# One core, three blocks of tokens: a group of gates moved to the start of the middle block, z's product and the stores of x tied to products

## Chip, cores and metric

The kernel runs on one core of one Trainium2 chip. The metric is the device time of one execution in microseconds; smaller is better. Five engines work side by side, each through its own instructions in order: TensorE (PE, with its weight loads PEld), VectorE (DVE), ScalarE (ACT), GpSimd (POOL) and SyncE (SP). Here SP only issues DMA transfers; POOL issues DMA transfers as well and computes a little.

## What is computed

One encoder layer runs over 2048 tokens of a prompt and 64 tokens of a second sequence that brings its own state. Cut to its core:

```python
h = rms_norm(x, g_pre)
vA, bA, cA, zA, q, f, iv, zB, gA, gB = split_cols(h @ w_in)       # ten times 1024 columns
yA = (silu(zA) * bA * causal_conv3(cA * vA)) @ w_a_out
fg = lb + (1 - lb) * sigmoid(f)                                   # 8 heads of 128
S, o = hgrn2_scan(S0, silu(q) * QK_SCALE, 1 - fg, iv, log(fg))    # chunks of 64 tokens
o = o * rsqrt(mean(o * o) + EPS) * g_onorm
yB = (o * silu(zB)) @ w_b_out
x = x + rms_norm((sigmoid(gA) * yA + sigmoid(gB) * yB) @ w_o, g_post)
x = x + (p @ w_ple_proj) * sigmoid(rms_norm(x, g_ple) @ w_ple_gate)
```

All data are fp32. The outputs are x for both sequences, the last two columns of the convolution's input, and the scan's final states.

## The kernel before

**Blocks.** The 2112 tokens are cut into three blocks of 768, 704 and 640 tokens, held with features on partitions. Every block goes through the same stages: the gates (columns gA and gB), `path_b` (eight heads with the scan), `path_a`, the merge, `out`, then the norms and the final gate. The stages of two blocks interlock: while TensorE works on the first seven groups of gates of the next block (`LEAD = 7`), the norms of the block just finished (`final_norm`, L1405) run on the other engines. Then come the finished block's final gate (`final_gate`, L1458) and after it the next block's `path_b` (L1213).

**Products.** An fp32 matrix is split into a high part `hi` (cast on ACT) and a rest `lo` (DVE, L226), and each matrix product is made of three fp32r matmuls (L442 to L444: hi by hi, hi by lo, lo by hi). `sgroup` (L427) works two 128-column blocks of weights against the halves of the token block in seven products instead of eight, with sums S1 to S4 of weight tiles as operands. A product is 12 matmuls, a group 84.

**Weights and their sums.** `combined` (L341) provides the operands. The first time that a pair of weight blocks is used, four raw tiles are loaded (L236), four sums are made on DVE (L352), split, and stored together with their `lo` parts, for later blocks (L331 for S, L280 for `low`). Later uses load sums and `lo` parts again (L236 and L274). Pools: 5 buffers for raw tiles, 4 for `hi`, 4 for `lo`, 3 for sums `s`. All loads, and these stores too, go through SP's queue, except that `stores[0]` is set to POOL's queue when block 1 begins (L1641). The last group of gates (gB, column blocks 6 and 7) has no sums after block 0, where it runs through another routine; block 1 is the first to make them.

**Gates.** `gates` (L868) is a generator of eight groups; each group writes two gate tiles, which POOL stores (L866). Seven groups are drawn before the final gate of the block before. In blocks 1 and 2 the eighth is drawn in `path_b`, after the preparation of head 5 (`hd == KH + 1`, L1223 to L1226), with SP as the queue of its stores for that moment.

**Hooks.** After every product, `hook` (L313) runs one entry of a list: a step of the attention, of a norm, or nothing. In `path_b` of blocks 1 and 2 a head is given 14 entries, one for each product of the next head's preparation, and 21 where the group of gates stands between. Steps of a head's attention sit at entries 2 to 10; at 11 the normalized output `o` goes out through the buffer `to` (L1055), at 14 it is read back in another order (L1060), and at 21 `scale_o` (L1209) multiplies it into z (L1211) and POOL stores z (L1218, kind `o`).

**Order on an engine.** The source gives dependencies and a rough order. A scheduler in the framework decides where an instruction stands in its engine's queue. `paced` (L300) adds a dependency on `last[0]`, the last matmul emitted so far, to an instruction.

**Norms.** `final_norm` loads x (L1418), adds the normalized `out` (L1436, L1437), takes the second mean square (L733, `rms` L715), and then, in eight steps `j` that stand two products apart, stores x of column block `j` for the final gate (L1447), multiplies by g_ple (L1454) and splits into `h2` (L226). `final_gate` reloads x and p (L1319), merges (L1463, L1464) and stores y (L1465). The large tiles come from one ring of 48 buffers (`rt`, L154).

Of the kernel before, what the change touches and what calls it, by code (L numbers as in the profile page):

```python
# [14 lines left out]
ALU = mybir.AluOpType  # L15
# [5 lines left out]
KB = D // P  # L21
KH = KB // 2
NH = 8
# [70 lines left out]
def hybrid_step(  # L94
# [17 lines left out]
    V, A, G, T, SP = nc.vector, nc.scalar, nc.gpsimd, nc.tensor, nc.sync  # L112
# [13 lines left out]
    def nm(s):  # L126
        uid[0] += 1
        return f"{s}_{uid[0]}"
# [12 lines left out]
    def sized(bl, steps):  # L141

        while True:
            with sized_to(bl):
                try:
                    made = next(steps)
                except StopIteration:
                    return
            yield made

    def hn():
        return width[0] // 2

    def rt(n=0, dt=F32):  # L154
        t = ring.tile([P, BN + 2], dt, tag="r", name=nm("r"))
        return t if n is None else t[:, : n or width[0]]
# [10 lines left out]
    def spill(kind, j):  # L167
        return dram.tile([P, BN], F32, tag=f"{kind}{j}", name=nm(kind), bufs=2)[:, : width[0]]
# [56 lines left out]
    def split(src, hi, lo):  # L225
        return A.copy(hi, src).ins, V.tensor_tensor(lo, src, hi.bitcast(F32), ALU.subtract).ins  # L226
# [12 lines left out]
    lows, turn, stores = {}, [0], [SP]  # L239
# [54 lines left out]
    last, hooks, copies, adds, ahead, evicted, freed, powers, means = [None], [], [None], [None], [], [], [], [], []  # L294
# [5 lines left out]
    def paced(dma):  # L300

        tc.add_manual_dep(
            dma.ins, last[0].name, mybir.DependencyInfo(mybir.DependencyClass.Sync, mybir.DependencyReason.DATA), reason="paced"
        )
# [410 lines left out]
    def rms(acc, out, segs, hasten=False):  # L715


        cols = [col_rstd(acc[:, cols_of(sg)], sg["n"]) for sg in segs]
        yield
        for sg, col in zip(segs, cols):  # L720
            if hasten:
                ahead[:] = [V.tensor_copy(out[:, cols_of(sg)], spread(col, sg["n"])).ins]
            else:
                A.copy(out[:, cols_of(sg)], spread(col, sg["n"]))
        yield

    def sum_squares(j, src, acc, n):
        if j == 0:
            A.activation(acc, src, AF.Square)
        else:  # L730
            sq = rt(n)
            A.activation(sq, src, AF.Square)
            V.tensor_tensor(acc, acc, sq, ALU.add)  # L733
# [134 lines left out]
    def gates(bl, hc, kept, first):  # L868


        groups = [(kind, j) for kind in (GA, GB) for j in range(0, KB, 2)]
        for kind, j in groups[: -1 if first else None]:
            outs = [rt(), rt()]
            n = groups.index((kind, j))
            sgroup(kind * 8 + j, kind * 8 + j + 1, hc, gate_sink(outs), first, by_k=n == 0 and not first, anew=n < LEAD)
            keep_gates(kept, kind, j, outs)
            yield
# [330 lines left out]

    def scale_o(d, hd):  # L1209
        z = d["z"][:, : d["npair"] * P].rearrange("q (g i a) -> q g i a", i=4, a=32)  # L1210
        V.tensor_tensor(z, d["ot"], z, ALU.mult)  # L1211

    def path_b(bl, hc, first, kept, fills, hs, lead_sums=None):  # L1213


        def keep_z(hd, z):
            kept["o", hd] = spill("o", hd)
            G.dma_start(kept["o", hd], z)  # L1218

        slots, base, d = {}, 0, None  # L1220
        for hd in range(NH):
            d = head_prep(bl, hc, hd, first, hs, d)
            if hd > 0 if first else hd == KH + 1:  # L1223
                queue, stores[0] = stores[0], SP
                next(fills, None)
                stores[0] = queue  # L1226
            assert not hooks
            attn = [head_attn(i, gs, d, hd) for i, gs in enumerate(bl["parts"])]
            keep = partial(keep_z, hd, d["z"])
            piece = lead_sums and partial(next, lead_sums, None)  # L1230

            def at(slot, *steps):
                slots.setdefault(base + slot, []).extend(s if callable(s) else partial(next, s) for s in steps if s is not None)

            if first:
                late = int(hd == 0)
                for g in attn:
                    for slot in (1 + late, 4, 7, 10, 13):
                        at(slot + late + (g is attn[1]), g)
                at(15 + late, keep)  # L1240
                for slot in (15, 17, 19) if hd else (17,):
                    at(slot, piece)
                if hd == NH - 1:
                    for slot in range(22, 70, 4):
                        at(slot, piece)
            else:
                pairs, one = attn[:2], attn[2:]
                for slot, steps in enumerate((pairs[:1], pairs[1:], one, one, pairs, one, pairs, (), one)):
                    at(slot + 2, *steps)
                at(11, partial(turn_o, d))  # L1250
                at(14, partial(read_o, d))
                at(14 + 7, partial(scale_o, d, hd), keep)
            count = 14 + 7 * (first or hd + 1 == KH + 1) if hd + 1 < NH else 1 + max(slots) - base
            for slot in range(base, base + count):
                steps = slots.pop(slot, None)
                hooks.append(partial(each, steps) if steps else None)
            base += count
# [147 lines left out]
    def final_norm(bl, segs, xo, acc, h2, kept, ask_ahead=False):  # L1405

        c = slice(segs[0]["off"], segs[-1]["off"] + hn())
        n = len(segs) * hn()  # L1410
        acc2, rs, rs2 = rt(), rt(), rt()
        xks = []

        def fetch():
            j = len(xks)
            if j < KB:
                xks.append(rt())
                G.dma_start(xks[j][:, c], x_fm[j * P : (j + 1) * P, segs[0]["t0"] : segs[0]["t0"] + n])  # L1418

        for _ in range(2 if bl["last"] else 4):  # L1420
            fetch()
        if kept is not None:
            for j in range(KB):
                sum_squares(j, xo[j], acc, width[0])
                if j % 2:
                    yield
        yield from rms(acc, rs, segs, bl["last"])
        if ask_ahead:
            for _ in range(3):
                fetch()  # L1430
                fetch()
                yield
        for j in range(KB):
            fetch()
            xj = xo[j][:, c]
            V.scalar_tensor_tensor(xj, xj, g_post[:, j : j + 1], rs[:, c], ALU.mult, ALU.mult)  # L1436
            V.tensor_tensor(xj, xj, xks[j][:, c], ALU.add)  # L1437

            for i in (j,) if not bl["last"] else (j - 1,) if 0 < j < KB - 1 else (j - 1, j) if j else ():
                sum_squares(i, xo[i][:, c], acc2[:, c], n)  # L1440
            yield
        yield from rms(acc2, rs2, segs, bl["last"])
        ts = []
        for j in range(KB):
            if kept is not None:
                kept["x", j] = spill("x", j)
                G.dma_start(kept["x", j], xo[j])  # L1447
            if len(h2) <= j:
                h2.append((rt(dt=F32R), rt(dt=F32R)))

            for i in (j, j + 1) if j == 0 else (j + 1,):
                if i < KB:
                    ts.append(rt())
                    V.scalar_tensor_tensor(ts[i][:, c], xo[i][:, c], g_ple[:, i : i + 1], rs2[:, c], ALU.mult, ALU.mult)  # L1454
            split(ts[j][:, c], h2[j][0][:, c], h2[j][1][:, c])
            yield
# [178 lines left out]
    fills = sized(blocks[0], gates(blocks[0], hc, kepts[0], True))  # L1635
    for bi, bl in enumerate(blocks):
        first, kept = bi == 0, kepts[bi]
        width[0] = bl["n"]
        segs = bl["segs"]
        if bi == 1:  # L1640
            stores[0] = G  # L1641
        ahead_of = (*range(W_A, W_A + KH), W_O, W_O + 1) if first else None
        path_b(bl, hc, first, kept, fills, hs if first else None, ahead_of and prepare_sums(ahead_of, pieces=True))
        run(fills)
        a = []
# [18 lines left out]
        mg, xo, h2, acc = [], [], [], rt()  # L1664
# [49 lines left out]
        if nxt:  # L1714
            xo.extend(stages[-1]["mid"])
            fills = sized(nxt, gates(nxt, hc, kepts[bi + 1], False))
# [65 lines left out]
```

## Time and profile before

| what | value |
|---|---|
| time, median of 3 runs | 2559.4 us (2559.28 to 2559.43) |
| the profiled execution's own time | 2566.42 us |
| its span, first to last instruction | 2564.2 us |
| TensorE busy | 2533.4 us (99%) |
| VectorE, ScalarE, GpSimd busy | 70%, 58%, 17% |
| DMA moved | 774.70 MB, mean 302 GB/s |
| block 1: first seven groups of gates; final gate of block 0 | about 894 to 988 us; about 988 to 1054 us |
| block 1: heads; the group of gates after head 5's preparation | about 1054 to 1368 us; about 1250 to 1270 us |
| block 2: first seven groups of gates | about 1737 to 1823 us |

Matmuls overlap in the pipeline, so that a matmul of 0.33 us may follow the one before by half of that. What counts for TensorE is the idle time ahead of a matmul, the number of matmuls in a stretch of time, and the clock that it was granted.

### The profile page before, as it was taken

To read this page: it belongs to the slowest core of one execution; us is meant where nothing else is said; L and a number is where in the kernel's file an instruction comes from. 1 tells how busy PE (TensorE), PEld (TensorE's weight loads), DVE (VectorE), ACT (ScalarE), POOL (GpSimd) and SP (SyncE) were. 2 spreads that over 40 slices of the span, in tenths; PEclk is the share of its full clock that TensorE was granted. 3 is DMA by queue.
4 is the path that set the end of the run, shared out by engine and by line. 5 is a ranking of instruction groups with operands and counts; after the bars stand their busy time and mean duration, and the time that the engine had idled before them with its cause. 6 is when DMAs were issued, how large, how long until landed. Compare 5 with 4: busy or idle time off the path is not lost. (4 is left out here: it accounts for less than half of the span.)

```text
span 2564.2 us, 47005 instructions
## 1 busy us (share of the span) xinstructions
PE 2533.4 (99%) x16070; PEld 2516.8 (98%) x16070; DVE 1795.1 (70%) x3549; ACT 1481.9 (58%) x2876; POOL 448.1 (17%) x793
## 2 busy tenths in 40 slices
PE   9999999999999999999999999999999999999999
PEld 9999999999999999999899999999999999999998
DVE  7888888898868775577574556887437766336967
ACT  6666666554453664466464555666446665446675
POOL 2011121230022021122122221102112221001011
PEclk9999999999999999999999999999999999999999
DMA  8789888998797888888888998998889999989986
GB/s 329 245 283 318 276 291 289 323 367 302 255 342 252 269 306 270 302 275 293 283 276 308 338 389 311 337 303 315 306 302 319 326 328 321 302 300 324 336 273 202
DMA packets 370399, 774.70 MB, mean 302 GB/s; under 512 B 45734, under 2 KB 50528, under 8 KB 370160
## 3 DMA queue, kind: packets, MB, share of 16 engines
q1 hardware_dynamic: 321840, 582.95, 66.8%
q0 software_dynamic: 48320, 188.75, 20.6%
q8 instruction: 126, 2.06, 0.3%
q14 instruction: 113, 0.93, 0.1%
HBM read 559.43 MB, written 212.10 MB: 301 GB/s over the span
## 5 line engine op out<-in xcount | busy, mean ns | idle before, releaser
L442 PE MATMUL pg<-r,hi 128*128 128x320 f32 (+2 forms) x3304 | 1082.3, 328 | 1.7 <-ACT hf L456 1.4
L443 PE MATMUL pg<-r,hi 128*128 128x320 f32 (+2 forms) x3304 | 1067.7, 323 | 0.0
L444 PE MATMUL pg<-r,lo 128*128 128x384 f32 (+2 forms) x2368 | 773.3, 327 | 10.6 <-DMA lo<-low 9.7
L273 ACT CAST hi<-raw 128x512 fp32r<-128x512 f32 x726 | 447.1, 619 | 498.4 <-PE pg L443 172.4
L442 PEld LDWEIGHTS pg<-r,hi 128*128 128x128 f32 x3304 | 623.4, 189 | 2.9 <-ACT hf L456 2.2
L443 PEld LDWEIGHTS pg<-r,hi 128*128 128x128 f32 x3304 | 623.1, 189 | 0.0
L444 PEld LDWEIGHTS pg<-r,lo 128*128 128x128 f32 x2368 | 445.6, 188 | 12.8 <-DMA lo<-low 11.5
L444 PE MATMUL pg<-r,s 128*128 128x320 f32 (+1 forms) x936 | 296.6, 317 | 3.0 <-DMA s<-low 3.0
L594 PE MATMUL pg<-r,hi 128*128 128x320 f32 (+2 forms) x864 | 277.2, 322 | 0.5 <-DVE r L226 0.4
L593 PE MATMUL pg<-r,hi 128*128 128x320 f32 (+2 forms) x864 | 274.9, 322 | 0.0
L226 ACT CAST hi<-raw 128x512 fp32r<-128x512 f32 x252 | 155.3, 620 | 157.8 <-PE pg L443 42.7
L226 DVE TENSOR_TENSOR r<-r,r 128x320 fp32r<-128x320 f32 (+7 forms) x350 | 206.3, 609 | 45.7 <-ACT r L226 44.2
L226 DVE TENSOR_TENSOR lo<-raw,hi 128x512 fp32r<-128x512 f32 x231 | 158.1, 687 | 80.5 <-ACT hi L226 76.3
L226 ACT CAST r<-r 128x320 fp32r<-128x320 f32 (+7 forms) x350 | 183.1, 556 | 43.8 <-DVE r L1333 8.4
L595 PE MATMUL pg<-r,lo 128*128 128x352 f32 (+2 forms) x564 | 181.0, 321 | 1.3 <-DMA lo<-low 1.2
L444 PEld LDWEIGHTS pg<-r,s 128*128 128x128 f32 x936 | 176.3, 188 | 4.0 <-DMA s<-low 3.9
L226 ACT CAST hi<-s 128x512 fp32r<-128x512 f32 x160 | 98.8, 618 | 137.6 <-PE pg L443 109.8
L632 PE MATMUL pg<-r,hi 128*128 128x384 f32 (+2 forms) x512 | 167.0, 327 | 0.2 <-DVE r L226 0.2
L631 PE MATMUL pg<-r,hi 128*128 128x384 f32 (+2 forms) x512 | 165.6, 327 | 0.2 <-ACT hi L273 0.2
L594 PEld LDWEIGHTS pg<-r,hi 128*128 128x128 f32 x864 | 162.2, 188 | 2.1 <-DVE r L226 1.6
L593 PEld LDWEIGHTS pg<-r,hi 128*128 128x128 f32 x864 | 161.2, 188 | 1.3 <-ACT r L226 0.8
L456 ACT COPY hf<-pg 128x352 f32<-128x352 f32 (+2 forms) x354 | 157.4, 446 | 2.6 <-PE pg L444 2.1
(394 smaller groups left out, 4109.6 us busy)
## 6 DMA issues: line engine op xcount, KB each, us to landing
raw<-w_blk SPq DMA_DIRECT2D x578, 256.0 KB, 4.4
raw<-S SPq DMA_DIRECT2D x440, 256.0 KB, 4.7
lo<-low SPq DMA_DIRECT2D x421, 256.0 KB, 4.4
s<-low SPq DMA_DIRECT2D x305, 256.0 KB, 4.6
low<-lo SPq DMA_DIRECT2D x275, 256.0 KB, 4.1
S<-s SPq DMA_DIRECT2D x156, 256.0 KB, 3.9
low<-r POOLq DMA_DIRECT2D x50, 256.0 KB, 5.2
r<-w_blk POOLq DMA_DIRECT2D x48, 256.0 KB, 7.1
```

What stands on the lines that cost most here:

```text
L226: return A.copy(hi, src).ins, V.tensor_tensor(lo, src, hi.bitcast(F32), ALU.subtract).ins
L273: A.copy(hi, raw)
L442: add(hi[:, k, :], xhi, start=start and k == 0, stop=False)
L443: add(hi[:, k, :], xlo, start=False, stop=False)
L444: last[0] = add(lo[:, k, :], xhi, start=False, stop=k == KH - 1).ins
L456: copied = A.copy(got[n], ps[bank])
L593: add(hi[:, k, :], xhi, start=start and k == 0, stop=False)
L594: add(hi[:, k, :], xlo, start=False, stop=False)
L595: last[0] = add(lo[:, k, :], xhi, start=False, stop=k == KH - 1).ins
L631: T.matmul(ps, hi[:, k % 4, :], xhi[:, c], start=k == ks[0], stop=False)
L632: T.matmul(ps, hi[:, k % 4, :], xlo[:, c], start=False, stop=False)
```

## The change

Three edits:

1. **Gates.** In block 1 the eighth group of gates is drawn ahead of head 0's preparation, right behind the final gate of block 0, again with SP as the queue of its stores. No head of block 1 has 21 entries any more. Block 2 keeps its group after head 5's preparation; its stores of sums do not exist, so the switch of queues there is dropped. Block 0 is unchanged.
2. **z.** The product of z and `o` in `scale_o` gets a dependency on the last matmul emitted before it (blocks 1 and 2).
3. **Stores of x.** In `final_norm` of blocks 0 and 1 each store gets such a dependency. At step 0 column blocks 0 and 1 are stored, at step `j` block `j + 1`; the steps stand two products apart.

```diff
     def scale_o(d, hd):
         z = d["z"][:, : d["npair"] * P].rearrange("q (g i a) -> q g i a", i=4, a=32)
-        V.tensor_tensor(z, d["ot"], z, ALU.mult)
+        paced(V.tensor_tensor(z, d["ot"], z, ALU.mult))
...
         slots, base, d = {}, 0, None
+        late_gates = KH + 1 if bl["last"] else None
+        if not first and not bl["last"]:
+            queue, stores[0] = stores[0], SP
+            next(fills)
+            stores[0] = queue
         for hd in range(NH):
             d = head_prep(bl, hc, hd, first, hs, d)
-            if hd > 0 if first else hd == KH + 1:
-                queue, stores[0] = stores[0], SP
+            if hd > 0 if first else hd == late_gates:
                 next(fills, None)
-                stores[0] = queue
...
-            count = 14 + 7 * (first or hd + 1 == KH + 1) if hd + 1 < NH else 1 + max(slots) - base
+            count = 14 + 7 * (first or hd + 1 == late_gates) if hd + 1 < NH else 1 + max(slots) - base
...
         for j in range(KB):
-            if kept is not None:
-                kept["x", j] = spill("x", j)
-                G.dma_start(kept["x", j], xo[j])
+            for i in () if kept is None else (0, 1) if j == 0 else (j + 1,):
+                if i < KB:
+                    kept["x", i] = spill("x", i)
+                    paced(G.dma_start(kept["x", i], xo[i]))
```

## Prediction

> **What bounds the kernel.** First the page's table of engines: busy time, share of the span, instructions.
>
> ```profile
> PE 2533.4 (99%) x16070; PEld 2516.8 (98%) x16070; DVE 1795.1 (70%) x3549; ACT 1481.9 (58%) x2876; POOL 448.1 (17%) x793
> ```
>
> TensorE is busy for all but 30.8 us of the 2564.2 us span, and the change adds and removes no matmul. So it can only win, or lose, idle time of TensorE and time at a lowered clock. Second, the view of waits for PE alone, columns "us in total, times, longest":
>
> ```profile
> PE pg L444 <- DMA lo<-low: 9.7, 4, 6.0
> PE pg L444 <- DMA s<-low: 3.0, 3, 1.3
> PE pg L442 <- ACT hf L456: 1.4, 1, 1.4
> PE pa L1097 <- DVE att L1119: 0.3, 1, 0.3
> PE pa L1111 <- DVE att L1119: 0.2, 1, 0.2
> ```
>
> One wait of 6.0 us stands out; most others are near 1 us. Third, the busy time by stretches of 10 us, first the old place of the moved group (columns: from:to, length, then busy us and instructions of PE, PEld, DVE, ACT, POOL, then PE's granted clock, DMA share, GB/s):
>
> ```profile
> 940.00:950.00 10.00, 10.00 (x64) 10.00 (x63) 6.03 (x10) 6.08 (x11) 1.62 (x3) 1.00 0.94 298
> ...
> 1250.00:1260.00 10.00, 7.03 (x41) 6.21 (x39) 8.85 (x16) 4.92 (x10) 2.92 (x5) 0.96 0.89 291
> 1260.00:1270.00 10.00, 6.62 (x24) 6.63 (x25) 1.70 (x5) 1.11 (x3) 0.71 (x1) 0.52 0.92 322
> ```
>
> The first row is the undisturbed rate in block 1: 64 matmuls in 10 us, 0.156 us each, so a product of 12 takes 1.87 us. In 1250 to 1270 us TensorE idles 2.97 + 3.38 = 6.35 us, and in the second stretch the clock is 0.52: its 24 matmuls fill 6.62 us where 24 x 0.156 = 3.75 would do. The stall costs 6.35 + 2.87 = **9.2 us**, not 6.0.
>
> **The gates' group.** Fourth, the timeline and SP's own waits at that place say why:
>
> ```profile
> 1254.68 0.72 SPq L274 DMA_DIRECT2D lo<-low  x1
> ...
> 1263.38 0.66 PE L444 MATMUL pg<-r,lo 128*128 128x352 f32 x1 [6.03 <-DMA lo<-low]
> ```
>
> ```profile
> SPq L236 <- DVE hf L994: 4.9, 1, 4.9
> SPq L280 <- DVE lo L226: 3.0, 2, 2.7
> ```
>
> TensorE waits from 1257.35 us for the `lo` part of the fifth product's weights. The load left SP at 1254.68 and landed at the end of the wait, 8.7 us later. Four products of 1.87 us before 1257.35 lies the group's start, 1249.9, so the buffer that the load reuses was free at 1251.7: the load left 3.0 us late. Ahead of it in SP's queue stood a load held 4.9 us by DVE's attention work (L994), and stores of `lo` parts held 3.0 us until DVE had made them (L226).
>
> The move takes all that the group issues to about 1054 us: 84 matmuls; seven loads (four raw tiles, three `lo` parts) and eight stores of 256 KB on SP; two stores of 352 KB on POOL; on DVE four sums and four splits. It removes nothing, so the matmuls cost the same. What counts is whether the load waits again. Before, head 0's first group stood there, also one that makes sums (two groups of DVE: busy us, mean ns, idle before; then DVE, SP and PE from the timeline; then the stretch):
>
> ```profile
> L352 DVE TENSOR_TENSOR s<-raw,raw 128x512 f32<-128x512 f32 x80 | 54.8, 686 | 9.5 <-DMA raw<-w_blk 6.6 <-DMA S<-s 2.7
> L226 DVE TENSOR_TENSOR lo<-s,hi 128x512 fp32r<-128x512 f32 x160 | 110.1, 688 | 52.1 <-ACT hi L226 44.5 <-DMA low<-lo 7.4
> ...
> 1053.96 0.69 DVE L226 TENSOR_TENSOR lo<-s,hi 128x512 fp32r<-128x512 f32 x1 [1.40 <-ACT hi L226]
> ...
> 1055.35 0.32 SPq L274 DMA_DIRECT2D lo<-low  x1
> ...
> 1061.56 0.43 PE L444 MATMUL pg<-r,lo 128*128 128x352 f32 x1
> ...
> 1060.00:1070.00 10.00, 9.87 (x61) 9.58 (x61) 4.36 (x9) 4.96 (x9) 1.08 (x2) 1.00 0.99 348
> ```
>
> There the same load left at 1055.35, landed in time but for 0.13 us (10.00 - 9.87), and the clock stayed at 1.00. Its stores went through POOL. In the built program of the changed kernel they stand on SP ahead of this load; the last of them needs the split that DVE ended at 1053.96 + 0.69 = 1054.65, before the load's buffer comes free. DVE is light there: 8 x 0.69 = 5.5 us of the group's work beside the merges. So the stores should not hold SP. Behind it comes head 0's own group with sums, now among gate stores. Bounds for the new place: 0.1 us (this row) and 9.2 us (the stall again). I take **1.0**, near the first: three `lo` loads in each of two groups, each about 6 us under way against 5.6 us of three products, a few tenths late at worst. Heads 5 to 7 lose the seven entries of pause; heads 1 to 4 go without them already. Gain: 9.2 - 1.0 = **8.2 us**.
>
> The clock, weighed: the Trainium skill, "TensorE: Matmul & The Clock Gate", Part 1, says that the clock falls to half after an idle window of about 3.4 us and returns after about as long busy. The row at 1260 agrees (0.52 after 6.03 us); the row at 930 in the next fence (0.83, longest wait 2.5 us) does not fit it. By the page the x stores below would win 3.6 us in block 0 where the rows give 5.3, and the sum would be 2550.1 us.
>
> **The stores of x.** The same view where they stand now, and where they go:
>
> ```profile
> 920.00:930.00 10.00, 8.95 (x57) 8.67 (x56) 7.62 (x12) 3.30 (x6) 1.08 (x2) 1.00 1.03 408
> 930.00:940.00 10.00, 7.50 (x37) 7.21 (x36) 5.86 (x9) 5.97 (x11) 1.63 (x3) 0.83 0.90 326
> ...
> 960.00:970.00 10.00, 10.00 (x64) 10.00 (x63) 7.73 (x11) 6.85 (x13) 0.54 (x1) 1.00 0.81 270
> 970.00:980.00 10.00, 10.00 (x65) 10.00 (x64) 7.88 (x12) 7.11 (x13) 1.08 (x2) 1.00 0.76 250
> ...
> 1770.00:1780.00 10.00, 9.29 (x62) 8.74 (x61) 5.92 (x10) 5.47 (x12) 2.06 (x4) 1.00 0.96 354
> ...
> 1800.00:1810.00 10.00, 10.00 (x70) 10.00 (x69) 7.81 (x13) 7.03 (x14) 0.00 (x0) 1.00 0.89 302
> 1810.00:1820.00 10.00, 10.00 (x71) 10.00 (x70) 7.44 (x11) 7.22 (x15) 1.08 (x2) 1.00 0.94 312
> ```
>
> ```profile
> x<-r POOLq DMA_DIRECT2D x8, 384.0 KB, 6.3
> ...
> POOL x L1447 <- DVE r L1437: 32.4, 13, 5.5
> ...
> 910.80 0.54 POOL L1447 DMA_DIRECT2D x<-r  x1 [3.14 <-DVE r L1437]
> ...
> 942.72 0.54 POOL L1447 DMA_DIRECT2D x<-r  x1 [5.51 <-DVE r L1437]
> ...
> 954.73 0.82 PE L700 MATMUL pa<-ident,cols 128*128 128x128 f32 x6
> 986.86 0.79 ACT L859 ACTIVATE r<-r 128x704 f32<-128x704 f32 x1
> ...
> 1793.68 0.54 PE L700 MATMUL pa<-ident,cols 128*128 128x128 f32 x3 [0.29 <-POOL cols L689]
> 1822.44 0.74 ACT L859 ACTIVATE r<-r 128x640 f32<-128x640 f32 x1 [0.61 <-DVE r L490]
> ```
>
> First row: eight stores, size, median us to landing. The row of waits says that POOL issues a store as soon as DVE has made the block (L1437), long before the steps in which the source puts it: the scheduler had moved them up. Eight of 384 KB, 3.1 MB, fall between 910 and 943 us, beside loads of x; there (920 row) the DMAs are full (408 GB/s, share 1.03) and TensorE waits 1.05 + 2.50 us for weights and runs 37 matmuls in 7.50 us (37 x 0.156 = 5.8): 3.55 + 1.7 = 5.3 us. Block 1 loses 0.7 (1770 row). With the tie the stores stand between the second norm's transposes (L700) and the seventh group's last sigmoid (L859): about 957 to 985 and 1797 to 1823 us. 3.1 MB in 28 us adds 110 GB/s: 270 + 110 = 380 in block 0; 2.9 MB in 26 us make 312 + 110 = 420 in block 1, as full as the 408 row. Price there: from 0 to 5.3 us a block; I take 1.0 in block 0 and 1.5 in block 1, near the 1770 row, which bore eight stores at 0.7. Net 6.0 - 2.5 = **3.5 us**.
>
> The new wait on POOL holds the gates' stores behind it (L866) and at the end the first reload of x (L1319), for which the merge on DVE waits; a store's product is done when its turn comes, so nothing for it. But in the built program the buffers of x blocks 4 and 5 are used again by `h2` (ACT) and that of block 6 by a gate tile (DVE): a store must land within about 4 products, 7.5 us; 6.3 fits.
>
> **z.** The last chain that reaches TensorE, in order of time:
>
> ```profile
> L1211 DVE TENSOR_TENSOR r<-r,r 128x640 f32<-128x640 f32 x16 | 13.2, 826 | 44.7 <-DMA r<-to 44.7
> ...
> 1157.23 0.83 DVE L1211 TENSOR_TENSOR r<-r,r 128x640 f32<-128x640 f32 x1 [3.28 <-DMA r<-to]
> ...
> 1378.37 0.83 DVE L1211 TENSOR_TENSOR r<-r,r 128x640 f32<-128x640 f32 x1 [6.81 <-DMA r<-to]
> ...
> 1379.66 0.50 ACT L923 ACTIVATE r<-hf 128x352 f32<-128x352 f32 x1 [7.11 <-DVE hf L483]
> ...
> 1381.06 0.43 PE L442 MATMUL pg<-r,hi 128*128 128x352 f32 x1 [1.35 <-ACT hf L456]
> ```
>
> Sixteen products of z stand too early on DVE and block it 44.7 us in total; twice that reaches TensorE: after 1378 through L483, ACT and PSUM (1.35 us), after 1157 through the mask copies L1119 (0.26 + 0.23, shown as 0.3 and 0.2). In the built program the tied products stand some 15 instructions later, among the next head's states, when the transfer has landed. Behind them wait those states and mask copies, and on POOL the store of z stands ahead of a reciprocal root of the attention (L689); a late product of TensorE would hold these, but TensorE is the engine that never waits long. Bounds: 1.8 gained; up to 1.4 lost, the dearest such row. I take **1.5**.
>
> **Sum.** 8.2 + 3.5 + 1.5 = 13.2 us. Every reordering shifts the DMA queues, and waits of about 1 us (s<-low: three in 3.0) come up at new places: 2.2 us given back. Forecast -11.0 us. Against the profiled execution that is 2566.4 - 11.0 = 2555.4; its own time stands 7.0 us above the median, so I put the difference on the median: 2559.4 - 11.0 = **2548.4 us**.
>
> **Rivals.**
> 1. *The stall goes along with the group* (the move doesn't do what it is placed for): SP's stores hold the `lo` load once at the new place. For it: the load has no slack there (0.13 us late already). Against it: DVE's splits ended before the load left. 8.2 falls away: -5.0 + 2.2 = -2.8, 2556.6 us.
> 2. *Two stalls instead of one* (slower): two groups with sums follow each other, and the stores of the first hold SP for the loads of both. It decides where the `lo` loads leave SP 3 us or more after the buffer is free, as at 1254.68. Price 2 x 9.2 - 9.2 = +9.2, with x and z -5.0 and +2.2 given back: +6.4, 2565.8 us. For it: both use SP and the same four `lo` buffers. Against it: head 0's stores go through POOL.
> 3. *The peak of x only moves*: the 420 GB/s in block 1 and 380 in block 0 cost what the old places did: 3.5 falls away, -7.5, 2551.9 us.
> 4. *Nothing comes back*: all three gains in full, 9.2 + 6.0 + 1.8 = 17.0: 2542.4 us.
>
> **Chances.** Forecast 0.55, rival 1 0.16, rival 2 0.12, rival 3 0.09, rival 4 0.08. A measurement of this kernel tells about 0.2% (5.1 us) from no change. Faster by more: 0.52 + 0.08 + 0.08 = 0.68; within: 0.03 + 0.16 + 0.01 = 0.20; slower 0.12. The range leaves out rival 2 and half of rival 4: 2542 to 2562 us.
>
> **What would show it.** Right: no wait of 6 us and no clock of 0.52 near 1260; at 1054 to 1082 us waits of under 1 us in all; 920 to 940 us at 64 matmuls a stretch; L1211 hardly waiting for `r<-to`; DMA rows near 1800 to 1820 above 400 GB/s. Wrong: a clock under 0.9 between 1054 and 1085 or 957 and 990 us, or ACT waiting for `x<-r`.

## The result, and the profile after

The changed kernel takes 2544.8 us (2541.6 to 2548.5); the kernel before, beside it on the same chip, takes 2559.3 us (2558.0 to 2560.3). The ratio is 0.9946 [0.9934, 0.9959], and 0.0054 x 2559.3 = **13.8 us less** (10.5 to 16.9). The forecast was 11.0 us less, 2548.4 us. The profiled execution of after took 2544.6 us, with a span of 2542.7 us. Against the span of before that is 21.5 us less, half as much again as the medians give, because the profiled execution of before stood 7.0 us above its median.

The page's table of engines of after, in the columns known from before:

```profile
PE 2527.4 (99%) x16070; PEld 2514.8 (99%) x16070; DVE 1794.5 (71%) x3549; ACT 1482.2 (58%) x2876; POOL 446.7 (18%) x793
```

The number of instructions is the same on every engine. TensorE is busy for 6.0 us less; 2.9 and 1.7 of these are the time at a lowered clock that the prediction read in the rows of 1260 and 930 us, and the rest is not followed. It idles for 2542.7 - 2527.4 = 15.3 us where 30.8 stood. The waits of PE alone (us in total, times, longest):

```profile
PE pa L700 <- POOL cols L689: 2.9, 5, 0.8
PE pg L444 <- DMA lo<-low: 2.0, 3, 1.0
...
PE pg L444 <- DMA s<-low: 0.7, 1, 0.7
```

The loads of `lo` cost 2.0 us instead of 9.7, those of `s` 0.7 instead of 3.0, and the wait for L456 is gone. The busy time by stretches of 10 us, first at the old place of the x stores and at their new one, then at the new and at the old place of the moved group:

```profile
920.00:930.00 10.00, 10.00 (x64) 10.00 (x63) 9.11 (x13) 7.36 (x13) 1.08 (x2) 1.00 0.85 275
930.00:940.00 10.00, 10.00 (x65) 10.00 (x64) 6.84 (x11) 5.95 (x11) 1.07 (x2) 1.00 0.82 275
970.00:980.00 10.00, 10.00 (x63) 10.00 (x62) 9.14 (x15) 7.09 (x12) 1.62 (x3) 1.00 0.98 342
1050.00:1060.00 10.00, 9.63 (x60) 9.34 (x59) 5.86 (x11) 4.66 (x9) 2.62 (x5) 1.00 0.90 328
...
1250.00:1260.00 10.00, 10.00 (x68) 10.00 (x67) 8.54 (x24) 6.90 (x13) 3.16 (x5) 1.00 0.91 308
1260.00:1270.00 10.00, 10.00 (x71) 9.98 (x70) 4.36 (x13) 3.57 (x8) 1.31 (x2) 1.00 1.01 351
...
1800.00:1810.00 10.00, 10.00 (x64) 10.00 (x63) 1.56 (x3) 2.34 (x5) 2.13 (x4) 1.00 1.01 393
```

Where the 920 and 930 rows of before had 57 and 37 matmuls, there are 64 and 65, and the clock is 1.00. The stretch from 1250 to 1270 us has no idle time. The moved group idles for 0.37 us in all, and 393 GB/s in block 1's new place of x cost nothing. On POOL, the stores now wait for products:

```profile
POOL x L1451 <- PE pg L444: 28.6, 10, 3.3
```

(L1451 is L1447 of before; the edits add three or four lines.) These agree with what the prediction said would show it right, and no wait of L1211 for `r<-to` is listed any more. One sign did not come: the DMA rows at 1800 to 1820 us, named as above 400 GB/s, are 393 and 299, and the peak of 403 stands ten us earlier.

### The profile page after: what moved, and what is told of

Read it like the earlier page. It is cut to its first block, busy times and chain, and to the rows that moved or that the text cites. A ratio compares the mean times of both kernels' runs of the same rounds, so it can differ in the third digit from the quotient of the medians.

```text
span 2542.7 us, 47020 instructions
## 1 busy us (share of the span) xinstructions
PE 2527.4 (99%) x16070; PEld 2514.8 (99%) x16070; DVE 1794.5 (71%) x3549; ACT 1482.2 (58%) x2876; POOL 446.7 (18%) x793
## 3 DMA queue, kind: packets, MB, share of 16 engines
q8 instruction: 126, 2.06, 0.3%
## 4 chain that ended last, share of the span: by engine, by line
PE 91%; issue 3%; DVE 3%; DMA 2%; ACT 0%; POOL 0%; SPq 0%; DVEq 0%; ACTq 0%; POOLq 0%
PE pg L442 20%; PE pg L444 20%; PE pg L443 20%; PE pg L594 4%; PE pg L593 4%; PE pg L595 4%; PE pg L633 3%; PE pg L632 3%; PE pg L631 3%; PE pa L1125 1%; PE pa L1165 1%; DMA lo<-low 1%; PE pa L1167 1%; PE pa L1111 1%; PE pa L1110 1%
## 5 line engine op out<-in xcount | busy, mean ns | idle before, releaser
L226 ACT CAST hi<-raw 128x512 fp32r<-128x512 f32 x252 | 155.3, 620 | 159.3 <-PE pg L443 41.9
L226 DVE TENSOR_TENSOR r<-r,r 128x320 fp32r<-128x320 f32 (+7 forms) x350 | 205.9, 607 | 45.4 <-ACT r L226 44.4
L226 DVE TENSOR_TENSOR lo<-raw,hi 128x512 fp32r<-128x512 f32 x231 | 157.8, 686 | 73.4 <-ACT hi L226 69.9
L226 ACT CAST r<-r 128x320 fp32r<-128x320 f32 (+7 forms) x350 | 182.8, 556 | 42.6 <-DVE r L1336 8.3
L226 ACT CAST hi<-s 128x512 fp32r<-128x512 f32 x160 | 98.9, 618 | 144.6 <-PE pg L443 116.9
L456 ACT COPY hf<-pg 128x352 f32<-128x352 f32 (+2 forms) x354 | 157.2, 446 | 2.1 <-PE pg L444 1.7
```

Of the source, the lines that this page charges most:

```text
L456: copied = A.copy(got[n], ps[bank])
```

## Experiments

**Theory.** Each of the three terms acts at its own place, so that single edits give their own part and the parts add up: gates about 8 us, x 3.5, z 1.5. **Rivals:** the parts don't add up, since a stall that goes uncovers the next; the gates' stall is made by their own stores in SP's queue, so that another queue would do as well as another place; the x stores gain by being spread or tied, not by their place, or they pay at the new place for what they save; z is hidden. Three groups of four kernels each ran with the kernel before beside them (medians of before 2559.92, 2560.72 and 2558.94 us). A difference in us is that of the ratio, with its 95% interval; the ratio is close to that of the means, and the difference of two medians can be up to 1.6 us off it.

### The parts one by one

**Gates alone** (the first edit on the kernel before):

```diff
+        late_gates = KH + 1 if bl["last"] else None
+        if not first and not bl["last"]:
+            queue, stores[0] = stores[0], SP
+            next(fills)
+            stores[0] = queue
...
```

> Only the group of gates of the middle block is moved; z and the stores of x as before. Theory A (three separate stalls, each removed by its own edit, sizes as in the sum): -8 us against the kernel before, no wait of 6 us at 1250 to 1270 us, no clock of 0.52 there, under 1 us of wait at the new place. Theory B (the gain is one thing, the move, and the ties bring nothing): -13 to -15 us here. Theory C (the stall comes and goes between executions, so the profile oversized it): -3 to -5 us.

2552.34 us, ratio 0.9967 [0.9954, 0.998]: **-8.4 us** (-11.8 to -5.1). The stretches of its trace at the x stores' old place and at the group's old place:

```profile
920.00:930.00 10.00, 7.94 (x50) 7.65 (x49) 7.99 (x11) 5.58 (x10) 2.16 (x4) 1.00 1.03 407
930.00:940.00 10.00, 10.00 (x53) 10.00 (x54) 6.28 (x9) 5.03 (x9) 1.08 (x2) 0.83 1.01 379
1250.00:1260.00 10.00, 10.00 (x65) 9.98 (x64) 8.48 (x28) 8.23 (x13) 3.91 (x6) 1.00 0.72 243
```

The gates' stall is gone and that of x stays as it was. At the new place 0.57 us are waited. The term of the sum was 8.2.

**Stores of x alone** (the third edit on the kernel before):

```diff
-            if kept is not None:
-                kept["x", j] = spill("x", j)
-                G.dma_start(kept["x", j], xo[j])
+            for i in () if kept is None else (0, 1) if j == 0 else (j + 1,):
+                if i < KB:
+                    kept["x", i] = spill("x", i)
+                    paced(G.dma_start(kept["x", i], xo[i]))
```

> Only the stores of x are tied and stand one step earlier in the source. Theory A: -3.5 us (2 to 5.5), 920 to 940 us back at 64 matmuls in 10 us, the 6 us wait at 1263 us still there. Theory B: within 1 us of the kernel before. Theory C (the full DMAs only move to 1790 to 1820 us): waits for s<-low or lo<-low of 2 us or more there, time within 1.5 us of before.

2552.87 us, ratio 0.9975 [0.9966, 0.9985]: **-6.4 us** (-8.7 to -3.8). Its stretches at the old place, at the new one, and at the gates:

```profile
920.00:930.00 10.00, 10.00 (x64) 10.00 (x63) 9.11 (x13) 7.34 (x13) 1.08 (x2) 1.00 0.83 282
...
960.00:970.00 10.00, 10.00 (x64) 10.00 (x64) 8.21 (x13) 6.82 (x13) 2.16 (x4) 1.00 1.04 395
...
1250.00:1260.00 10.00, 6.62 (x32) 6.62 (x33) 4.07 (x7) 2.40 (x4) 0.79 (x1) 0.83 0.99 358
...
1800.00:1810.00 10.00, 10.00 (x68) 10.00 (x67) 6.32 (x10) 6.67 (x12) 1.08 (x2) 1.00 1.04 406
```

The gates' stall stays. At the new places the DMAs are as full as at the old one (395 and 406 GB/s, shares of 1.04), and TensorE waits for nothing. Counting matmuls from the start of the trace, this profile gains 5.6 us on before between the 5200th and the 5600th matmul (block 0's stores) and 2.6 us between the 10400th and the 11200th (block 1's); 2.7 us of its lead stand ahead of any edit and differ from run to run.

**z alone** (the second edit on the kernel before), and **all but z** (the changed kernel without this edit):

```diff
-        V.tensor_tensor(z, d["ot"], z, ALU.mult)
+        paced(V.tensor_tensor(z, d["ot"], z, ALU.mult))
```

> Only z's product is tied. Theory A: -1.5 us (0.5 to 2); L1211 waits for r<-to under 5 us in total instead of 44.7; no wait of 1.35 us for ACT hf L456; the 6 us wait at 1263 us still there. Theory B: within 0.5 us of before, L1211's waits gone all the same.

> The changed kernel without the tie of z. If the tie of z is worth nothing measurable (as it was alone), the time is that of the changed kernel, -13 to -15 us against the kernel before. If it is worth the 1.5 us of the sum once the other stalls are gone, -12 to -13 us, with TensorE waiting 1 to 1.5 us for ACT hf L456 near the end of the middle block's heads.

z alone takes 2559.90 us, ratio 0.9999 [0.9991, 1.0008]: -0.3 us (-2.3 to +2.0). In the waits of DVE the row of L1211, 44.7 us in before, is gone, and PE's wait for L456 too. What PE still waits for with z alone:

```profile
PE pg L444 <- DMA lo<-low: 8.3, 5, 4.7
...
PE pg L444 <- DMA s<-low: 1.7, 2, 1.1
```

All but z takes 2546.53 us, ratio 0.9948 [0.9935, 0.9962]: -13.3 us (-16.6 to -9.7), the same as with z. So z does what it says and is worth nothing that these runs can tell, at most about 2 us.

The three parts make -8.4 - 6.4 - 0.3 = -15.1 us against -13.8 measured together: within their intervals they add up.

### What makes the gates' stall

**Old place, stores through POOL.** The queue's switch is left out of the kernel before, so that the late group's stores of sums stand in POOL's queue:

```diff
-                queue, stores[0] = stores[0], SP
                 next(fills, None)
-                stores[0] = queue
```

> The kernel before with one difference: the late gates' sums and low parts are stored through POOL, not SP; the group stays after head 5's preparation. If the stores that wait in SP's queue are what made the load of the low part late (3.0 us of SP's waits at L280 and more at L331), the load leaves in time and the stall of 6 us and the low clock are gone: -7 to -9 us. If it is the raw loads that DVE's attention work holds (4.9 us at L236), the load still leaves about 1 to 3 us late: 0 to -4 us. If POOL's queue holds the stores behind the attention's transfers, the sums' buffers come free late and the time is that of before or worse by up to 9 us.

2563.92 us, ratio 1.0014 [1.0002, 1.0025]: **+3.6 us**. The stall stays, 6.73 us by the timeline of PE:

```profile
1262.20 0.66 PE L444 MATMUL pg<-r,lo 128*128 128x352 f32 x1 [6.73 <-DMA lo<-low]
```

No store stands ahead of SP's loads any more, and SP waits all the same (SP's waits from 1245 to 1258 us), for the sums of DVE (L352), which free the raw tiles' buffers, and for a store of a sum that has to land before the buffer is loaded again. Just ahead of these it waits 5.5 us for the attention's work on DVE (L994), as it does in before (4.9):

```profile
SPq L236 <- DVE s L352: 4.2, 1, 4.2
SPq L274 <- DMA S<-s: 3.4, 1, 3.4
```

**After head 2's preparation** instead of head 5's:

```diff
-            if hd > 0 if first else hd == KH + 1:
+            late_gates = KH + 1 if bl["last"] else 2
+            if hd > 0 if first else hd == late_gates:
...
```

> The kernel before with the middle block's last gates after head 2's preparation instead of head 5's, stores on SP. If the stall comes from attention work and its transfers beside a group that makes sums, it is there at any head: within 3 us of the kernel before, a wait of 4 to 7 us for lo<-low and a low clock near 1160 us. If something of head 5 alone makes it, it is gone: -7 to -9 us.

2563.19 us, ratio 1.0012 [1.0, 1.0024], +3.1 us (0.0 to +6.1). The stall moves along, to 1160.70 us:

```profile
PE pg L444 <- DMA lo<-low: 10.7, 4, 7.0
```

**Late groups without stores.** In blocks 1 and 2 the last group makes its sums and keeps none; so the stores of these sums and `lo` parts are left out, and block 2 makes them again:

```diff
+        if stores[0] is None:
+            return split_w(s)
...
-                queue, stores[0] = stores[0], SP
+                queue, stores[0] = stores[0], None if not first else SP
```

> The kernel before with the late group of gates at its old place, but without its eight stores of sums and low parts; so the last block's group makes its sums again and stores none either. If the stores' share in the full DMAs makes the low part's load land 8.7 us after issue, it lands in 4 to 6 us, and the wait near 1263 us falls from 6 to 1 to 3 us with the clock at 1.00: -4 to -8 us, less up to 3 us if the last block's group now waits too. If the lateness of the raw loads and sums behind DVE's attention work is enough, the wait stays at 4 us or more and a second one appears in the last block: 0 to +9 us.

2560.62 us, ratio 1.0003 [0.9994, 1.0012]: no difference. Block 1's wait is shorter, and block 2 has one of its own (two lines of PE's timeline; this kernel's lines stand two further). Counting matmuls from the start of the trace, this profile gains 3.5 us on before at block 1's group and loses 4.9 at block 2's:

```profile
1255.25 0.66 PE L446 MATMUL pg<-r,lo 128*128 128x352 f32 x1 [2.65 <-DMA lo<-low]
...
2052.45 0.39 PE L444 MATMUL pg<-r,hi 128*128 128x320 f32 x1 [1.78 <-DVE r L1029]
```

**New place, stores through POOL** (the changed kernel without the switch):

```diff
-            queue, stores[0] = stores[0], SP
             next(fills)
-            stores[0] = queue
```

> The changed kernel with the moved group's stores on POOL instead of SP. The prediction's step said that the stores on SP do not hold the loads at the new place: then this is within 2 us of the changed kernel, -12.5 to -16.5 us. If SP's stores cost there, 1 to 3 us faster; if POOL's queue, busy with y and the reloads, holds the sums' buffers, 2 to 9 us slower with a wait for lo<-low near 1055 us.

2545.91 us, ratio 0.9949 [0.9936, 0.9961]: as the changed kernel. Its wait at the new place is 1.56 us (1058.14) against 0.37.

**What these groups have in common** is read at the one `lo` load that ends TensorE's longest wait. First the view of DMA issues (size, median us from issue to landing). After, at the new place (1046 to 1056 us); the first row is packets and rate of that stretch:

```profile
DMA packets 1453, 3.14 MB, mean 314 GB/s; under 512 B 187, under 2 KB 187, under 8 KB 1451
...
lo<-low SPq DMA_DIRECT2D x3, 256.0 KB, 3.9
```

Before, at the old place (1249 to 1258 us):

```profile
DMA packets 908, 2.20 MB, mean 244 GB/s; under 512 B 118, under 2 KB 118, under 8 KB 907
...
r<-tv POOLq DMA_DIRECT2D x1, 320.0 KB, 7.1
r<-tk POOLq DMA_DIRECT2D x1, 320.0 KB, 8.0
...
lo<-low SPq DMA_DIRECT2D x1, 256.0 KB, 8.7
```

With stores through POOL at the old place (1249 to 1258 us), and after head 2 (1148 to 1156 us):

```profile
lo<-low SPq DMA_DIRECT2D x2, 256.0 KB, 7.7
```

```profile
lo<-low SPq DMA_DIRECT2D x1, 256.0 KB, 9.8
```

The 3.9 us are a median of three loads (3.5, 5.4 and 3.9 us). The one that TensorE waited for, in the sixth product of the group, took 5.4 (timelines of SP and PE):

```profile
1050.05 0.44 SPq L274 DMA_DIRECT2D lo<-low  x1
...
1055.54 0.43 PE L444 MATMUL pg<-r,lo 128*128 128x352 f32 x1 [0.37 <-DMA lo<-low]
```

The four `lo` buffers take turns, one for each product. So the buffer for this load came free when the product four before its own ended, and the load is needed three products and two matmuls later: 6.1 us at the new place, 6.9 to 8.2 us at the old ones, where short waits stretch the products. The table sets beside each other how long after its buffer came free the load left SP, and how long it took to land:

| the `lo` load that TensorE waited for | left after its buffer was free, us | landing, us | buffer free to load needed, us | longest wait of TensorE, us |
|---|---|---|---|---|
| new place in before (head 0's group) | 0.0 | 6.2 | 6.1 | 0.13 |
| new place (after) | 1.0 | 5.4 | 6.1 | 0.37 |
| new place, stores on POOL | 1.0 | 6.6 | 6.1 | 1.56 |
| old place, no stores | 3.4 | 6.1 | 6.9 | 2.65 |
| old place, before | 4.3 | 8.7 | 6.9 | 6.03 |
| old place, stores on POOL | 6.5 | 7.6 | 7.5 | 6.73 |
| after head 2 | 5.3 | 9.8 | 8.2 | 6.98 |

A wait is the first number plus the second less the third, within 0.2 us. Landing alone would have made waits of 1.8 us at most (8.7 - 6.9 in before); the larger part of every long wait is that SP issues the load late. In the four kernels of the table with the group among the heads, SP waits 4.9 to 6.2 us for the attention's work on DVE (L994) just ahead of the group, and then for the group's own sums, splits or stores; at the new place the wait for L994 is missing and the load leaves at most 1.0 us late. The group's stores add to both parts (3.4 and 6.1 us without them, 4.3 and 8.7 with them), but without them the stall is still there. Which of SP's waits makes how much of the lateness is not separated. The rate tells nothing of it: 244 GB/s where a load takes 8.7 us, 314 where it takes 5.4. At the old place the attention's transfers of `tk`, `tv` and `to` through POOL stand beside the loads, and they are absent at the new one. That they are what stretches the landing is argued from the place, not shown: no kernel took them away alone.

**Block 2's group early too:**

```diff
-        late_gates = KH + 1 if bl["last"] else None
-        if not first and not bl["last"]:
+        late_gates = None
+        if not first:
```

> The changed kernel with the last block's eighth group of gates also ahead of its head 0. That group makes no sums and shows no wait of TensorE after head 5 in the changed kernel, so nothing is left to win there: within 2 us of the changed kernel, -12.5 to -16.5 us. A further gain of 3 us or more would say that heads of the last block lose time to the group too; a loss of 3 us or more that the pause of seven products was needed there.

2545.53 us, ratio 0.9941 [0.9928, 0.9953]: the same as the changed kernel. Block 2 has no stores of sums, and its group had no stall to lose. No version beat the changed kernel by more than the intervals.

### What the x stores gain by: place, spread, or tie

**Tied, each at its own step** (no store a step early):

```diff
-                G.dma_start(kept["x", j], xo[j])
+                paced(G.dma_start(kept["x", j], xo[j]))
```

> The kernel before with the stores of x tied to products at their own step j, not one step earlier. Theory A (the full DMAs at 910 to 940 us are the whole cost, any later place will do): as with both edits, -6 to -7 us. Theory D (the step matters, because the ring's buffers of x are written again two products, 3.7 us, after the last stores instead of four, while a store takes about 6 us to land): ACT or DVE wait for x<-r by 2 to 3 us for each of the last two blocks of x, in both blocks; if that reaches TensorE through PSUM the gain shrinks to -2 to -5 us, if PSUM's banks cover it the gain stays.

2555.06 us, ratio 0.9984 [0.9976, 0.9993]: -4.1 us (-6.1 to -1.8). Waits for the stores' buffers hardly come up (one `x<-r` wait of 1.4 us on DVE). The interval overlaps that of the x edit as it is, so whether the early step adds to the tie stays open.

**All eight at step 0, tied to one product:**

```diff
-            if kept is not None:
-                kept["x", j] = spill("x", j)
-                G.dma_start(kept["x", j], xo[j])
+            for i in range(KB if kept is not None and j == 0 else 0):
+                kept["x", i] = spill("x", i)
+                paced(G.dma_start(kept["x", i], xo[i]))
```

> The kernel before with all eight stores of x issued together at step 0 behind the second norm, tied to one product. Burst theory (a backlog of transfers makes loads land late, whatever the rate over 10 us): 3.1 MB at once are about 8 us of the DMAs, loads issued behind them land 10 us or more after issue instead of 5 to 6, TensorE waits 3 to 8 us for weights near 955 to 965 and 1780 to 1795 us with a lowered clock; the time is that of before or up to 8 us worse. Place theory (only the place beside the first norm's loads was bad): no such waits, -5 to -7 us as with the spaced stores.

2555.35 us, ratio 0.9989 [0.998, 0.9997]: -2.8 us (-5.1 to -0.8), about half of what the spread stores gain, though the intervals overlap. POOL issues the eight in 4.26 us, and the loads behind them are slow (POOL's timeline, then the DMA issues of 950 to 965 us):

```profile
949.84 4.26 POOL L1447 DMA_DIRECT2D x<-r  x8
```

```profile
x<-r POOLq DMA_DIRECT2D x8, 384.0 KB, 7.0
...
s<-low SPq DMA_DIRECT2D x2, 256.0 KB, 10.2
```

TensorE waits only 0.77 us for them in block 0 (967.93), and with its surroundings loses 1.2 us there against the spread stores. In block 1 this profile gains the same 2.6 us on before as theirs. A further 2.3 us are lost against before near 1372 us, far from any store, in a wait for L456 of 2.27 us. So one profile shows a burst to cost about 1 us, in block 0; the rest of the difference is not settled.

**At the old place, tied and spread** (the store goes into the loop that makes the block):

```diff
             V.tensor_tensor(xj, xj, xks[j][:, c], ALU.add)
+            if kept is not None:
+                kept["x", j] = spill("x", j)
+                paced(G.dma_start(kept["x", j], xo[j]))
...
```

> The kernel before with each store of x tied to a product in the step of the first loop that makes its block, so at the old place but two products apart. Burst theory: spacing is what counts, loads near 920 to 930 us land in 6 to 8 us instead of 12 to 13, and most of the gain of the stores comes, -3 to -7 us. Place theory (loads of x, the gates' stores and the weights leave no room there): the wait of 2 to 3 us for lo<-low and the low clock near 930 us stay, within 2 us of before.

2556.23 us, ratio 0.9993 [0.9984, 1.0002]: -1.8 us (-4.1 to +0.5). The stall stays, 2.62 us at 928.48 (stretches of its trace):

```profile
920.00:930.00 10.00, 7.38 (x43) 7.09 (x42) 6.16 (x10) 5.47 (x10) 2.16 (x4) 0.95 1.03 404
930.00:940.00 10.00, 10.00 (x57) 10.00 (x57) 7.55 (x11) 5.31 (x10) 1.08 (x2) 0.88 0.95 335
```

The rate is that of the new place with no wait, but the loads land later. The DMA issues of this kernel at the old place (912 to 930 us), then of the x edit alone at the new one (955 to 975 us):

```profile
s<-low SPq DMA_DIRECT2D x3, 256.0 KB, 9.9
raw<-w_blk SPq DMA_DIRECT2D x3, 256.0 KB, 10.6
lo<-low SPq DMA_DIRECT2D x2, 256.0 KB, 9.4
```

```profile
raw<-w_blk SPq DMA_DIRECT2D x8, 256.0 KB, 5.4
s<-low SPq DMA_DIRECT2D x2, 256.0 KB, 5.9
...
lo<-low SPq DMA_DIRECT2D x2, 256.0 KB, 6.1
```

Here it is the landing that makes the wait, other than in the group of gates: the load that TensorE waits for at 928.48 left SP at 916.29 and took 12.1 us, and the one of before, at 933.43, left at 920.08 and took 13.3. So the place is most of the gain, 6.4 - 1.8 = 4.6 of 6.4 us (the intervals just overlap): the stores, tied and spread at the old place, leave the stall there. That it is the loads of x that leave them no room is argued from the place, not shown.

## Why the prediction was right, point by point

- **The gates' 8.2 us:** right; alone they gave 8.4, with 0.4 to 0.6 us waited at the new place for the 1.0 priced. The mechanism, a `lo` load that leaves SP late behind attention work, is what the runs show. Two readings of it were off. The load was not 3.0 but 4.3 us late: the prediction took four undisturbed products back from the wait, and by the timeline of PE the first product ended at 1250.4. And the part given to the stores in SP's queue does not hold: without them in that queue the load leaves 6.5 us late and the stall is as long; without them anywhere 2.65 us are left.
- **The new place was likened to head 0's group of before.** That held (0.13 us of waiting there, 0.37 in after). The step "the stores should not hold SP" did not: in after, SP's waits from 1044 to 1056 us show stores of `lo` parts (L280) that wait for DVE (L226) three times, 7.0 us in total and 3.6 at the longest. The load that TensorE waited for is not behind one of these waits; it left 1.0 us late, behind a load of a raw tile that waited 1.0 us for ACT (L456). So what rivals 1 and 2 needed, this load held by SP's stores or held for 3 us or more, did not come up.
- **The stores of x, 3.5 us:** the mechanism was right and the size too small; 6.4 (3.8 to 8.7) were measured. The term that failed is the price of 2.5 us at the new places, read from their 380 and 420 GB/s against the 408 of the stall. They ran at 395 to 406 and TensorE waited for nothing. Rival 3 failed for the same reason. The gross gain in one profile was 5.6 us in block 0 (5.3 forecast) and 2.6 in block 1, where the 0.7 of the 1770 row alone was too little: the profile gains 1.25 us at that row, 0.75 near 1790 and the rest before.
- **z, 1.5 us:** the waits went as said (44.7 us of DVE, and the wait for L456), but no time can be seen to follow: -0.3 us, -2.3 to +2.0, which leaves 1.5 possible. The wait was not a chance of one execution: in the profiles of this case it is there in all ten kernels without the tie, from 0.50 us (all but z) to 2.35 (after head 2), and in none of the four with it. What is not shown is the step from this wait to time; whether it is lost again elsewhere stays open.
- **The 2.2 us given back:** 1.4 us can be followed in block 2 in the two profiles. The sum without that item, 13.2, is nearest to the 13.8 measured; 8.2 + 3.5 + 1.5 - 2.2 came out 2.8 us short mainly through x. No row stood behind the 2.2 as such; the parts measured alone exceed the whole by 1.3. That the sum came this near is in part luck: x was 2.9 us too small, and z, by its middle value, 1.2 too large.
- **Putting the difference on the median** and not on the profiled execution was right: spans differ by 21.5 us, medians by 14.5.
- **The clock:** the rule of the Trainium skill, "TensorE: Matmul & The Clock Gate", Part 1, on which the prediction drew, would have made the x term smaller, with 3.6 us instead of 5.3 in block 0. The measurement goes the other way: one profile gains 5.6 us there, and the clock fell after shorter waits than the rule has (last section).

## What to carry to other kernels

Before a group of work is moved or a queue is blamed, take the one load that the engine waits for and read three times: when its buffer came free, when the load left its queue, and when it landed. Here the gates' load had 6.1 to 8.2 us, took 5.4 to 9.8 to land and left 0 to 6.5 us late, and only the sum explains the wait; the load behind the x stall took 12.1 to 13.3 us to land. A median over several loads can hide the load that matters (3.9 against 5.4 us), and the rate in GB/s does not tell it. Spreading transfers in a place without room gained 1.8 us where moving them gained 6.4. That a wait of 1 to 2 us goes, even in every profile, is no forecast of time: z's wait went, and the time did not show it.

## What the runs showed of the hardware

A short idle time of TensorE can cost twice. After 1.78 us of waiting, which ended at 2052.45 (late groups without stores, PE's timeline), the matmuls run at full speed for 0.8 us and then take 0.47 us instead of 0.31 and follow each other by 0.27 us instead of 0.15, until 3.2 us later (2053.27 to 2056.47):

```profile
2052.97 0.31 PE L444 MATMUL pg<-r,hi 128*128 128x320 f32 x1
2053.12 0.36 PE L445 MATMUL pg<-r,hi 128*128 128x320 f32 x1
2053.27 0.47 PE L446 MATMUL pg<-r,lo 128*128 128x320 f32 x1
...
2056.21 0.47 PE L445 MATMUL pg<-r,hi 128*128 128x320 f32 x1
2056.47 0.39 PE L446 MATMUL pg<-r,lo 128*128 128x320 f32 x1
2056.71 0.31 PE L444 MATMUL pg<-r,hi 128*128 128x320 f32 x1
```

After 1.56 us (stores through POOL at the new place) the clock stays:

```profile
1058.14 0.43 PE L444 MATMUL pg<-r,lo 128*128 128x352 f32 x1 [1.56 <-DMA lo<-low]
1058.41 0.33 PE L442 MATMUL pg<-r,hi 128*128 128x352 f32 x1
1058.58 0.32 PE L443 MATMUL pg<-r,hi 128*128 128x352 f32 x1
```

Over the profiles of this case, after their first 100 us, single waits of 1.78 us and more were followed by 9 to 19 matmuls that came every 0.27 or 0.29 us instead of every 0.15 or 0.16, for 2.8 to 5.8 us. They cost 1.3 to 2.8 us on top of the wait. There is one exception (2.35 us at 1379.16, after head 2), and after no single wait up to 1.60 us did it happen. So the same 2 us of waiting are worth 2 us or 3 to 4. The Trainium skill, "TensorE: Matmul & The Clock Gate", Part 1, gives about 3.4 us both for the idle window that lowers the clock and for the busy one that restores it. The 3.2 us of slow matmuls are near the second, with 2.8 to 5.8 us over all profiles; the drops after 1.78, 2.06 and 2.27 us do not agree with the first.

Landing times of 256 KB loads on SP's queue lay between 3.9 and 10.6 us as medians in the rows above. The fastest of the some 1700 such loads of a profile, after its first 100 us, took 2.5 to 2.6 us in every profile of this case, the slowest 12.1 to 15.1. The Trainium skill, "DMA: Bandwidth & Descriptors", Anatomy of one DMA (SWDGE path), has a fit of 2.0 us plus the bytes at 436 GB/s for one DMA issued through GpSimd; for 256 KB that is an estimate of 2.6 us. The loads here go through SP and not through GpSimd; their fastest agree with it, and most take longer.

**Still open:** what of the landing time beside an attention comes from which transfer, and how the late issue divides among SP's waits; the rest of what the burst loses; whether the early step of x adds to its tie; whether the wait that z's tie removes is worth any time.
